# A two-layer hybrid encoder on one core: shared q and k roots, S5 work moved from GpSimd to VectorE, a bias negated on ScalarE, and one SBUF offset for the large buffers

## The chip, the cores and the metric

The kernel runs on one core of a Trainium2 chip. The metric is the device time of one execution in microseconds (us), as the median of the runs shown. The engines are named as the profile names them: PE (TensorE matmul), PEld (its weight loads), DVE (VectorE), ACT (ScalarE), POOL (GpSimd), SP (SyncE, which issues the DMAs). The span is the time from the first to the last instruction of the profiled execution.

## The reference, cut to what matters

Two layers, each a feed-forward block (FFN), a mixer and another FFN, on 512 tokens of width 1024, in float32:

```python
for layer in range(DEPTH):
    x = x + 0.5 * swiglu(rms_norm(x, ffn1_norm[layer]), ffn1_w_in[layer], ffn1_w_out[layer])
    x = x + hybrid_mixer(rms_norm(x, mix_norm[layer]), w_in[layer], ...)
    x = x + 0.5 * swiglu(rms_norm(x, ffn2_norm[layer]), ffn2_w_in[layer], ffn2_w_out[layer])
```

The mixer projects the normed x once and gives the columns to four groups: A (windowed attention, 4 query and 2 key heads), B (a bidirectional S5 scan over 16 groups with 64 complex states each, then a gate), C (dilated attention, 4 heads) and D (neighbourhood attention with a learned relative bias, 4 heads). A, C and D normalise each 64-wide head of q and k by its root mean square. The four outputs are multiplied by `w_out` and added to x.

```python
o_a, lse_a = banded_attention(rms_norm(heads(aq), qk_gain[0]), rms_norm(heads(ak), qk_gain[1]), heads(av), ...)
y_b = s5_bidirectional(bu, lam_re, lam_im, log_step, b_re, b_im, c_re, c_im, d_skip)
g = jax.nn.gelu(y_b)
y_b = g * jax.nn.sigmoid(g @ w_glu)
o_c = dilated_attention(rms_norm(heads(cq), qk_gain[2]), rms_norm(heads(ck), qk_gain[3]), heads(cv), ...)
o_d = neighborhood_attention(rms_norm(heads(dq), qk_gain[4]), rms_norm(heads(dk), qk_gain[5]), heads(dv), rel_bias)
return concat([o_a, y_b, o_c, o_d]) @ w_out
```

## The kernel before, in words

**Tiling.** The 512 tokens lie along the free dimension, features on the 128 partitions. Every float32 operand of a large matmul is split into a high and a low part, and `mm3` (L106 to L109) makes three matmuls of one product: low weight by high data or the other way round (L107, L108), and high by high (L109). A weight tile `wr` (up to 128x1024) is loaded by SP; `weights` (L118) splits it into `wh` (a cast on ACT, L125) and `wl` (a subtraction, L126, on DVE in the FFNs and on POOL in the mixer, where it is called with `pooled`).

**The FFNs.** The normed input is in eight pairs `hh`, `hl` (high, low). `pgp` and `pup` are the gate and up products into PSUM, `a` is the activated pair, `pop` the product with the output weights.

**The mixer.** `project` makes the 256-column blocks of the projection (`ppr`, 128x256 per matmul) from `wh`, `wl` and `hh`, `hl`; `ppt` is the transposed product for S5's input u and D's v. `qk` is one of six streams (dq, dk, cq, ck, aq, ak). Its fourth step ends in `norm`: ACT copies the block to `q` (L575) and squares it to `sq` (L579), DVE sums per head into `ss` (L580), adds epsilon (L583), takes 1/sqrt in `rsqrt` (L137; eleven small operations of 128x16, L140 to L145, three rounds of L143, L144, L145) and multiplies `q` by it (L589, four times 128x256). The fifth step, `flip`, transposes `q` on PE (`ptp`, L599); ACT scales and copies the result as the high part `o` (L606, L608), DVE makes the low part (L613, `kl` for k). `attention` has a first step (scores `psc` on PE, L687 and L688; bias and row minimum on DVE, L690; exp on ACT, L692; the division on POOL, L704) and a second (transposes L723, `pT` on ACT and DVE, L725 and L726, products `pot`, L728 and L729). After two heads, `m` is split into the pair `mt`: high on ACT (L746), low on POOL (L747). `merge` multiplies `mt` by the output weights (`pop`, L107 to L109) and DVE adds to `x` (L769). `d_bias` loads one head's bias for D (SP, L787) and makes mask minus bias of it with three DVE operations (L794).

**S5.** `s5` is a generator with a `yield` after each step: input rotation (`per`, `pei`, L818; two halves), scans (L833, L835), output rotation (L842 to L847, two halves; the products `rot` of L843 and L846 are on POOL, the other four on DVE), output matmuls `pyp` (L857 to L859, two halves of 24), and the gate (`gsp`, `pzp`, `mt` at L895).

**What sets the order.** `ORDER` (L35) is a list of tokens that gives the order in which steps are written: `dq` is the next step of stream dq, `Ds` and `Dt` the next halves of D's `first` and `second`, `s5` the next step of the generator, `mD` a step of the merge of D. Each step's instructions go to the engines' queues, and each queue runs in its order. A scheduler sets the final order from the written one, so the order on an engine is not read from the list alone. PSUM gives 3 banks to products (`mm`), 2 to scores and S5 (`sc`), 2 to transposes (`tp`) and 1 to `pot`.

## Time and profile before

| | before |
|---|---|
| median of 3 runs | 2018.51 us (2018.3 to 2020.4) |
| the profiled execution's own time | 2017.22 us |
| its span | 2015.4 us |
| mean granted clock of PE | 0.989 of full speed |
| PE busy | 1954.5 us (97%) |
| DVE, ACT, POOL busy | 1238.3, 801.1, 368.3 us |
| DMA | 189.5 MB, mean 94 GB/s |

Both layers have the same course. In the first, FFN 1 takes the span up to about 388 us, the mixer 388 to 643 us, FFN 2 the rest up to about 985 us; the second follows some 1000 us later. Times of places below are microseconds from the start of the span. An engine is busy while an instruction of it runs; matmuls overlap, so that a busy PE is one that never runs dry and not one at its peak rate.

### The profile page before, as it was taken

The page shows a single profiled execution, that of the slowest core. Times are in us where ns is not written, and L with a number is a line of the kernel's source. Part 1 is how long each engine was busy: PE and PEld are TensorE (multiplying, and loading weights), DVE is VectorE, ACT ScalarE, POOL GpSimd, SP SyncE. Part 2 cuts the span into 40 slices and gives each one's busy share as a digit, 9 for nine tenths or more (in the row PEclk, how much of TensorE's full clock was granted, in tenths as well). Part 3 has the DMA queues.
Part 4 walks back from the last instruction along what each step waited for, and adds up shares of the span by engine and source line. Part 5 has one row for each costly group of instructions (what it writes and reads, how often), then busy time and mean ns, then how long its engine had stood idle before and what let it go on. Part 6 is the DMA issues. An engine that isn't in the chain of part 4 may idle for free.

```text
span 2015.4 us, 25901 instructions
## 1 busy us (share of the span) xinstructions
PE 1954.5 (97%) x9656; PEld 1639.0 (81%) x9656; DVE 1238.3 (61%) x2317; ACT 801.1 (40%) x1515; POOL 368.3 (18%) x349
## 2 busy tenths in 40 slices
PE   8999999998999999999999999999989989999999
PEld 6788878897977888888888888788978768888887
DVE  6865547567797545445677655465787875444454
ACT  5333323453676323233432333234537753232332
POOL 4010100254455000000120101003544540000000
PEclk9999999998999999999999999999989999999999
DMA  4233343331312332323233332423313122333233
GB/s 177 81 102 91 105 94 101 99 116 47 98 55 72 102 97 92 102 84 110 84 116 92 99 93 94 107 90 106 112 45 93 50 71 89 100 96 102 81 108 104
DMA packets 75471, 189.50 MB, mean 94 GB/s; under 512 B 17984, under 2 KB 23872, under 8 KB 75344
## 3 DMA queue, kind: packets, MB, share of 16 engines
q1 hardware_dynamic: 75248, 187.77, 30.7%
q8 instruction: 76, 1.25, 0.3%
q14 instruction: 51, 0.42, 0.1%
q0 software_dynamic: 96, 0.07, 0.0%
...
## 4 chain that ended last, share of the span: by engine, by line
PE 81%; DVE 10%; ACT 4%; issue 2%; DMA 1%; POOL 1%; SPq 0%; DVEq 0%; ACTq 0%; POOLq 0%
PE pop L107 9%; PE pop L109 9%; PE pop L108 8%; PE pgp L107 7%; PE pgp L109 7%; PE pgp L108 7%; PE pup L107 7%; PE pup L109 7%; PE pup L108 7%; PE ppr L107 1%; PE ppr L108 1%; DVE wl L126 1%; PE ppr L109 1%; DMA wr<-in_f_w 1%; DVE hl L186 1%
## 5 line engine op out<-in xcount | busy, mean ns | idle before, releaser
L125 ACT CAST wh<-wr 128x512 fp32r<-128x512 f32 (+2 forms) x718 | 405.2, 570 | 962.6 <-PE pgp L109 306.4
L126 DVE TENSOR_TENSOR wl<-wr,wh 128x512 fp32r<-128x512 f32 (+2 forms) x618 | 408.6, 665 | 383.6 <-ACT wh L125 381.9
L107 PE MATMUL pop<-a,wl 128*128 128x512 f32 x704 | 277.9, 397 | 7.0 <-DVE wl L126 6.8
L107 PE MATMUL pgp<-hh,wl 128*128 128x512 f32 x704 | 275.3, 391 | 8.4 <-DVE wl L126 8.4
L107 PE MATMUL pup<-hh,wl 128*128 128x512 f32 x704 | 275.6, 392 | 2.7 <-DVE wl L126 2.7
L108 PE MATMUL pgp<-hl,wh 128*128 128x512 f32 x704 | 275.7, 392 | 2.5 <-DVE hl L186 2.4
L109 PE MATMUL pop<-a,wh 128*128 128x512 f32 x704 | 276.9, 393 | 0.0
L108 PE MATMUL pop<-a,wh 128*128 128x512 f32 x704 | 275.1, 391 | 0.6 <-DVE a L257 0.6
L109 PE MATMUL pup<-hh,wh 128*128 128x512 f32 x704 | 274.8, 390 | 0.0
L108 PE MATMUL pup<-hl,wh 128*128 128x512 f32 x704 | 274.8, 390 | 0.0
L109 PE MATMUL pgp<-hh,wh 128*128 128x512 f32 x704 | 274.4, 390 | 0.0
L196 POOL TENSOR_TENSOR t<-t,sq 128x512 f32<-128x512 f32 x42 | 60.0, 1430 | 658.2 <-ACT sq L195 656.9
L107 PEld LDWEIGHTS pop<-a,wl 128*128 128x128 f32 x704 | 132.6, 188 | 37.1 <-DVE wl L126 9.2
L107 PEld LDWEIGHTS pgp<-hh,wl 128*128 128x128 f32 x704 | 132.4, 188 | 36.4 <-DVE wl L126 8.8
L108 PEld LDWEIGHTS pgp<-hl,wh 128*128 128x128 f32 x704 | 132.4, 188 | 34.4 <-DVE hl L186 7.3
L126 POOL TENSOR_TENSOR wl<-wr,wh 128x512 fp32r<-128x512 f32 (+1 forms) x100 | 131.0, 1315 | 160.6 <-ACT wh L125 122.9
L107 PEld LDWEIGHTS pup<-hh,wl 128*128 128x128 f32 x704 | 132.4, 188 | 32.3 <-DVE wl L126 4.8
L109 PEld LDWEIGHTS pop<-a,wh 128*128 128x128 f32 x704 | 132.6, 188 | 30.5
L108 PEld LDWEIGHTS pop<-a,wh 128*128 128x128 f32 x704 | 132.6, 188 | 30.1 <-DVE a L257 1.0
L109 PEld LDWEIGHTS pup<-hh,wh 128*128 128x128 f32 x704 | 132.3, 188 | 27.6
L108 PEld LDWEIGHTS pup<-hl,wh 128*128 128x128 f32 x704 | 132.3, 188 | 27.6
L109 PEld LDWEIGHTS pgp<-hh,wh 128*128 128x128 f32 x704 | 132.3, 188 | 27.3
...
## 6 DMA issues: line engine op xcount, KB each, us to landing
...
bias<-in_ctab SPq DMA_DIRECT2D x8, 448.0 KB, 3.3
bias<-in_rbx SPq DMA_DIRECT2D x8, 448.0 KB, 4.1
...
```

Source lines behind the costliest of these rows:

```text
L107: nc.tensor.matmul(out, ll, rh, start=start, stop=False)
L108: nc.tensor.matmul(out, lh, rl, start=False, stop=False)
L109: nc.tensor.matmul(out, lh, rh, start=False, stop=stop)
L125: nc.scalar.copy(hi[:, :w], r)
L126: (nc.gpsimd if pooled else nc.vector).tensor_tensor(lo[:, :w], r, f32(hi[:, :w]), op=ALU.subtract)
L186: stt(hl, x[c], gcol, f32(hh), op0=ALU.mult, op1=ALU.subtract)
L196: gtt(acc, acc, sq, op=ALU.add)
```

## The change

What it does:

- `rsqrt` works on one flat tile of up to 32 columns. Of a pair (dq and dk, cq and ck, aq and ak) the `norm` of q ends at the sums; the `norm` of k adds its own sums beside them, takes one root for both (32, 32 and 24 columns) and multiplies q's and k's rows by it. `flip` of q therefore stands behind `norm` of k.
- In S5's output rotation the two products `rot` of each half (L843, L846) move from POOL to DVE, and so does the low part of `mt` (L747).
- `d_bias` no longer subtracts on DVE. The mask is in the loaded table as −1e30, and ACT negates the tile in one 128x896 operation (L802 of the changed kernel). The tile `dmask` and its load go.
- In `ORDER` S5's output matmuls come later and some steps of dq, aq, mD, mB and mC move.
- Before all other tiles, dummy tiles named `lay` and the eight x tiles are allocated in an order which puts all the large buffers (t2, k4, s8, wr, wh, wl, hh, hl, x) at addresses of 128 bytes above a multiple of 2048 in each partition. Before, wr and x lay at 992, t2, hh, hl, wh and wl at 1536, and k4 and s8 (which hold `a`, `mt`, `o`, `kl`, `pT`, `v`) at 1600 above one.

The number of matmul rows on PE is the same but for six; DVE has 68 fewer rows, POOL 21 fewer, ACT 6 more, SP as many. The core of the diff:

```diff
 ORDER = """
-dq dq dq dk dk dq dq dk s5 dk dv cq dk s5 Ds dv dv ck cq ck Ds cq dv Ds dv Ds Ds s5 cq s5 Dt ck s5 Dt s5 Dt ck
-cq s5 Ds cv Dt aq cv s5 aq Ds Dt Dt Ds ck Cs cv Dt s5 cv aq ak aq Cs s5 ak Dt Cs aq Cs Ct ak mD ak Cs Ct Cs Cs
-Ct ak Cs Ct s5 mD Ct mD As Ct As Ct Ct As mD As As At As As mB At As At At At mC mC mB mB mC At At mC At mC mC
+dq dq dq dk dk dq dk s5 dk dq dv cq dk s5 Ds dv dv ck cq ck Ds cq dv Ds dv Ds Ds s5 cq s5 Dt ck s5 Dt s5 Dt ck
+cq Ds cv Dt s5 aq cv aq s5 Ds Dt Dt Ds ck Cs cv Dt s5 cv aq ak aq Cs s5 ak Dt Cs Cs Ct ak mD ak aq Cs Ct Cs Cs
+Ct ak Cs s5 Ct mD Ct As Ct As Ct Ct As mD As As At As As mD At As At mB At At mB mB mC mC mC At At mC At mC mC
 mC mB mC mA mA
 """
...
+    t2("lay")
+    k4([P, 1024], name="lay")
+    s8([P, 2048], name="lay")
+    for tag, cols in (("wr", 1024), ("wh", 512), ("wl", 512), ("hh", 512), ("hl", 512)):
+        pool.tile([P, cols], F32 if tag == "wr" else F32R, tag=tag, bufs={"wr": 2, "hh": 8, "hl": 8}.get(tag, 4), name=nm(tag))
+    x = [pool.tile([P, S], F32, name=f"x{c}") for c in range(KC)]
...
-                sn = ss[:, :, :nh]
-                tt(sn, sn, bc(ec, 2, nh), op=ALU.add)
-                rn = sml([P, 4, 4], "rn")
-                rsqrt(rn[:, :, :nh], sn, [4, nh])
-                for j in range(2):
-                    for b in range(2):
-                        a = raw[j][:, b].rearrange("p (h d) -> p h d", d=64)
-                        tt(a, a, bc(rn[:, 2 * j + b, :nh], 2, 64), op=ALU.mult)
+                tt(ss, ss, bc(ec, 2, nh), op=ALU.add)
+                pair["raw"].append((raw, nh, o0))
+                if gi % 2 == 0:
+                    return
+                n = o0 + 4 * nh
+                rn = sml([P, 32], "rn")
+                rsqrt(rn[:, :n], pair["ss"][:, :n], n)
+                for rows, heads, o in pair["raw"]:
+                    rv = rn[:, o:o + 4 * heads].rearrange("p (b h) -> p b h", b=4)
+                    for j in range(2):
+                        for b in range(2):
+                            a = rows[j][:, b].rearrange("p (h d) -> p h d", d=64)
+                            tt(a, a, bc(rv[:, 2 * j + b], 2, 64), op=ALU.mult)
...
-                    gtt(mt[:, 1], m, f32(mt[:, 0]), op=ALU.subtract)
+                    tt(mt[:, 1], m, f32(mt[:, 0]), op=ALU.subtract)
...
-            for c0, m0, nk in ((0, 0, 2), (256, 2, 3), (640, 5, 2)):
-                bv = b[:, c0:c0 + nk * P].rearrange("p (k u w) -> p k u w", u=8, w=16)
-                tt(bv, bc(dmask[:, m0:m0 + nk], 2, 8), bv, op=ALU.subtract)
+            act(b[:, :896], b[:, :896], AF.Copy, scale=-1.0)
...
-                gtt(a, cz(si, gs), cz(T["s"], gs), op=ALU.mult)
+                tt(a, cz(si, gs), cz(T["s"], gs), op=ALU.mult)
...
-                gtt(b, cz(sr, gs), cz(T["s"], gs), op=ALU.mult)
+                tt(b, cz(sr, gs), cz(T["s"], gs), op=ALU.mult)
```

How it moves instructions. The first place is PE at the first scores of D in layer 0, where dk's transposes (`ptp` from `q_3656` before, `q_3624` after) come ahead of the scores `psc`. Before:

```order
1942 L599 MATMUL ptp_3758<-ident,q_3661 128x2x4x16
1943 L818 MATMUL pei_3774<-u_3323,s_624 128x64
1944 L107 MATMUL ppt_3694<-hh_3119,wl_3576 128x512
...
1955 L109 MATMUL ppt_3694<-hh_3153,wh_3575 128x512
1956 L107 MATMUL ppr_3717<-wh_3690,hl_3052 128x256
...
1967 L109 MATMUL ppr_3718<-wh_3690,hh_3085 128x256
1968 L687 MATMUL psc_3806<-o_3748,o_3554 128x256
1969 L687 MATMUL psc_3812<-o_3748,o_3554 128x384
```

and of the changed kernel:

```order
1967 L108 MATMUL ppr_3710<-wl_3683,hh_3091 128x256
1968 L109 MATMUL ppr_3710<-wh_3682,hh_3091 128x256
1969 L609 MATMUL ptp_3735<-ident,q_3624 128x2x4x16 x2
1970 L609 MATMUL ptp_3735<-ident,q_3629 128x2x4x16 x2
1971 L609 MATMUL ptp_3750<-ident,q_3624 128x2x4x16 x2
1972 L609 MATMUL ptp_3750<-ident,q_3629 128x2x4x16 x2
1973 L697 MATMUL psc_3796<-o_3740,o_3661 128x256
1974 L697 MATMUL psc_3802<-o_3740,o_3661 128x384
1975 L698 MATMUL psc_3796<-kl_3741,o_3661 128x256
1976 L698 MATMUL psc_3802<-kl_3741,o_3661 128x384
1977 L697 MATMUL psc_3931<-o_3740,o_3661 128x384
...
1981 L107 MATMUL ppt_3834<-hh_3014,wl_3702 128x512
```

The 12 `ppt` and 12 `ppr` that stood between dk's transposes and the scores stand ahead of the transposes now.

The second place is ACT at the same point; `o` are the scaled copies of the transposes, `a` the copy of a `ppt` bank, `wh` the weight casts of later projections. Of the changed kernel:

```order
280 L616 ACTIVATE o_3740<-ptp_3735,qkg 64x512
281 L618 ACTIVATE o_3740<-ptp_3735,qkg 64x512
282 L802 ACTIVATE bias_3791<-bias_3791 128x896
283 L616 ACTIVATE o_3755<-ptp_3750,qkg 64x512
284 L618 ACTIVATE o_3755<-ptp_3750,qkg 64x512
285 L802 ACTIVATE bias_3998<-bias_3998 128x896
286 L658 COPY a_3820<-ppt_3686 128x512
287 L702 ACT_TABLE_LOAD
...
291 L702 ACTIVATE p_3940,ll_3795<-p_3940,mn_3794 128x256
292 L802 ACTIVATE bias_4047<-bias_4047 128x896
293 L125 CAST wh_3849<-wr_3847 128x512
```

The negations of the first three heads' biases (L802) are new here, between the copies and ahead of the casts; before, the queue went from the copies `o` and `a` straight to the exponentials and casts.

The third place is DVE at the a pair's root, which the changed kernel runs between two additions of D's merge to `x` (L779, the former L769):

```order
664 L779 TENSOR_TENSOR x_72<-pop_5029,x_72 128x512
665 L585 TENSOR_REDUCE ss_4840<-sq_5077 128x4
666 L587 TENSOR_TENSOR ss_4840<-ss_4840,ec_3320 128x8
667 L700 ISA p_5129,mn_5124<-psc_5126,bias_5122 128x512
...
669 L139 TENSOR_SCALAR rn_5081<-ss_4840 128x24
670 L140 TENSOR_SCALAR rn_5081<-rn_5081 128x24
671 L142 TENSOR_TENSOR rq_5082<-rn_5081 128x24
...
678 L143 SCALAR_TENSOR_TENSOR rq_5082<-rq_5082,ss_4840 128x24
679 L779 TENSOR_TENSOR x_73<-pop_5302,x_73 128x512
680 L144 SCALAR_TENSOR_TENSOR rn_5081<-rq_5082,rn_5081 128x24
```

Rows 669 to 678 are ten operations of the root. The next product on PE, `pop_5310`, waits for row 679: the gate's two `pzp` hold the other two product banks. Before, the root of ak alone stood among the additions, with one of them and two `pT` between its operations.

## Rows read from the trace of the kernel before

**Rows 1.** The page: busy time, and the chain that ended last.

```profile
PE 1954.5 (97%) x9656; PEld 1639.0 (81%) x9656; DVE 1238.3 (61%) x2317; ACT 801.1 (40%) x1515; POOL 368.3 (18%) x349
...
PE 81%; DVE 10%; ACT 4%; issue 2%; DMA 1%; POOL 1%; SPq 0%; DVEq 0%; ACTq 0%; POOLq 0%
```

**Rows 2.** Stretches: length, busy time (count) of PE, PEld, DVE, ACT, POOL, clock, DMA.

```profile
300.00:350.00 50.00, 50.00 (x222) 41.36 (x221) 35.55 (x80) 16.28 (x27) 0.00 (x0) 1.00 0.33 104
...
450.00:500.00 50.00, 41.32 (x279) 39.51 (x278) 39.04 (x64) 19.43 (x45) 22.75 (x24) 0.86 0.16 53
```

**Rows 3.** Waits of PE in the mixer of layer 0: total, times, longest.

```profile
PE pyp L859 <- DVE zi L847: 5.7, 1, 5.7
PE pot L729 <- DVE pT L726: 2.9, 4, 1.2
...
PE pop L107 <- ACT mt L895: 1.6, 1, 1.6
PE pop L108 <- POOL mt L747: 1.2, 2, 0.9
```

**Rows 4.** PE at S5's output: start, us; in brackets the idle time before.

```profile
487.50 0.69 PE L859 MATMUL pyp<-zi,s 128*128 128x64 f32 x2 [5.68 <-DVE zi L847]
```

**Rows 5.** DVE in order of time there: start, us, line, output and inputs.

```profile
480.90 1.23 DVE L141 TENSOR_SCALAR rn<-rn 128x16 int32<-128x16 int32 x1
...
484.61 1.19 DVE L145 SCALAR_TENSOR_TENSOR rn<-rq,rn 128x16 f32<-128x16 f32 x1
485.83 0.17 DVE L143 TENSOR_TENSOR rq<-rn 128x16 f32<-128x16 f32 x1
486.04 0.17 DVE L144 SCALAR_TENSOR_TENSOR rq<-rq,ss 128x16 f32<-128x16 f32 x1
...
486.76 0.68 DVE L847 TENSOR_TENSOR zi<-zi,rot 128x512 f32<-128x512 f32 x1
```

**Rows 6.** POOL in order of time in the same stretch.

```profile
480.80 1.30 POOL L846 TENSOR_TENSOR rot<-sr,k 128x512 f32<-128x512 f32 x1
...
484.51 1.25 POOL L846 TENSOR_TENSOR rot<-sr,k 128x512 f32<-128x512 f32 x1
```

**Rows 7.** The stretch at the lower clock.

```profile
485.60:502.60 17.00, 15.10 (x71) 15.03 (x72) 9.78 (x26) 6.33 (x11) 0.16 (x1) 0.50 0.04 14
```

**Rows 8.** ACT in order of time at D's first scores.

```profile
438.18 0.69 ACT L606 ACTIVATE o<-ptp,qkg 64x512 fp32r<-64x512 f32 x1 [2.90 <-PE ptp L599]
438.88 0.69 ACT L608 ACTIVATE o<-ptp,qkg 64x512 fp32r<-64x512 f32 x1
...
444.46 0.59 ACT L648 COPY a<-ppt 128x512 f32<-128x512 f32 x1
```

**Rows 9.** PE in the same stretch.

```profile
437.65 0.61 PE L599 MATMUL ptp<-ident,q 128*128 128x128 f32 x4
...
438.23 0.47 PE L107 MATMUL ppt<-hh,wl 128*128 128x512 f32 x1
...
442.51 0.46 PE L687 MATMUL psc<-o,o 128*128 128x256 f32 x2
```

**Rows 10.** Groups by line and shape: count, busy us, mean ns, idle before.

```profile
L747 POOL TENSOR_TENSOR mt<-m,mt 128x512 fp32r<-128x512 f32 x12 | 16.4, 1364 | 33.2 <-ACT mt L746 33.2
...
L144 DVE SCALAR_TENSOR_TENSOR rq<-rq,ss 128x16 f32<-128x16 f32 x30 | 12.1, 404 | 0.8
```

**Rows 11.** DMA issues: count, KB, median us to landing.

```profile
bias<-in_rbx SPq DMA_DIRECT2D x8, 448.0 KB, 4.1
```

**Rows 12.** PE in FFN 2 of layer 0, first and last of 65 matmuls in sequence.

```profile
692.70 0.39 PE L109 MATMUL pup<-hh,wh 128*128 128x512 f32 x1
...
707.20 0.39 PE L107 MATMUL pgp<-hh,wl 128*128 128x512 f32 x1
```

**Rows 13.** PE there, first and last of 64 matmuls in sequence.

```profile
912.55 0.39 PE L109 MATMUL pop<-a,wh 128*128 128x512 f32 x1
...
926.97 0.39 PE L109 MATMUL pop<-a,wh 128*128 128x512 f32 x1
```

More of the change, by code (lines that the diff above doesn't have):

```diff
@@ L134, in weights, with rsqrt @@
         return at
-    def rsqrt(y, v, shape):
-        w = sml([P, 16], "rq")
-        w = w[:, :shape[0]] if len(shape) == 1 else w.rearrange("p (a b) -> p a b", a=shape[0])[:, :, :shape[1]]
+    def rsqrt(y, v, n):
+        w = sml([P, 32], "rq")[:, :n]
         yi = y.bitcast(I32)
@@ L156, in hybrid_encoder @@
     nc.sync.dma_start(gains, t["gains"])
-    x = []
     warm = pool.tile([P, 2], F32, name="warm")
@@ L160, in hybrid_encoder @@
     for c in range(KC):
-        xc = pool.tile([P, S], F32, name=f"x{c}")
-        nc.sync.dma_start(xc, t["xt"][c])
-        x.append(xc)
+        nc.sync.dma_start(x[c], t["xt"][c])
         if c == 0:
@@ L168, in hybrid_encoder @@
     sink = pool.tile([P, DEPTH, 4], F32, name="sink")
-    dmask = pool.tile([P, 7, 16], F32, name="dmask")
-    for tl, nme in ((qkg, "qkg"), (sink, "sink"), (dmask, "dmask")):
+    for tl, nme in ((qkg, "qkg"), (sink, "sink")):
         nc.gpsimd.dma_start(tl, t[nme])
@@ L560, in then, with qk @@
             return ld, go
-        def qk(blk0, nh, perm, gi, res, extra=None):
+        def qk(blk0, nh, perm, gi, res, pair, extra=None):
             st, steps = project(blk0)
@@ L570, in norm @@
                     extra(pts)
-                ss = sml([P, 4, 4], "ss")
+                if gi % 2 == 0:
+                    pair["ss"] = sml([P, 32], "ss")
+                    pair["raw"] = []
+                o0 = 16 * (gi % 2)
+                ss = pair["ss"][:, o0:o0 + 4 * nh].rearrange("p (b h) -> p b h", b=4)
                 for j in range(2):
@@ L900, in mixer @@
         dqk, dv, cqk, cv, aqk, av = [], [], [], [], [], []
+        pd, pc, pa = {}, {}, {}
         streams = {
-            "dq": qk(2, 4, 1, 4, dqk), "dk": qk(4, 4, 1, 5, dqk), "dv": v_perm(6, dv),
-            "cq": qk(8, 4, 0, 2, cqk), "ck": qk(10, 4, 0, 3, cqk), "cv": v_proj(12, cv),
-            "aq": qk(14, 4, 0, 0, aqk), "ak": qk(16, 2, 0, 1, aqk, lambda pts: av.append(v_split(pts, 128, 2))),
+            "dq": qk(2, 4, 1, 4, dqk, pd), "dk": qk(4, 4, 1, 5, dqk, pd), "dv": v_perm(6, dv),
+            "cq": qk(8, 4, 0, 2, cqk, pc), "ck": qk(10, 4, 0, 3, cqk, pc), "cv": v_proj(12, cv),
+            "aq": qk(14, 4, 0, 0, aqk, pa), "ak": qk(16, 2, 0, 1, aqk, pa, lambda pts: av.append(v_split(pts, 128, 2))),
             "s5": s5(), "mD": merge("woD", mt_d, 2), "mB": merge("woB", mt_b, 2), "mC": merge("woC", mt_ca, 3),
@@ L971, in _tables @@
         ctab[i] = np.where(mult > 0, slopes[4 + i] * dist - np.log(np.maximum(mult, 1)), BIG)
-    dmask = np.zeros((P, 7, 16), np.float32)
+    seen = np.zeros((P, 896), bool)
     ri = np.zeros((P, 896), np.int64)
@@ L975, in _tables @@
     r, c = np.arange(P) // 16, np.arange(P) % 16
-    for qb, k0, k1, col, m0 in ((0, 0, 2, 0, 0), (1, 0, 3, 256, 2), (3, 2, 4, 640, 5)):
+    for qb, k0, k1, col in ((0, 0, 2, 0), (1, 0, 3, 256), (3, 2, 4, 640)):
         qc = 16 * qb + c
@@ L983, in _tables @@
                     j = col + (kb - k0) * P + u * 16 + w
-                    dmask[:, m0 + kb - k0, w] = np.where((kc >= ws) & (kc < ws + 16), 0.0, BIG)
+                    seen[:, j] = (kc >= ws) & (kc < ws + 16)
                     ri[:, j] = u - r + 7
                     ci[:, j] = np.clip(kc - qc + 15, 0, 30)
-    return atab, ctab, dmask, ri, ci
+    return atab, ctab, seen, ri, ci
 def _layout(i):
@@ L1049, in _layout @@
     a["s5d"] = sd.reshape(DEPTH, P, 2 * P)
-    a["atab"], a["ctab"], a["dmask"], ri, ci = _tables()
-    a["rbx"] = ac(np.asarray(i["na_rel_bias"])[:, :, ri, ci])
+    a["atab"], a["ctab"], seen, ri, ci = _tables()
+    a["rbx"] = ac(np.where(seen, np.asarray(i["na_rel_bias"])[:, :, ri, ci], np.float32(-BIG)))
     return a
```

3 lines of the change are left out of this document (2 added, 1 removed).

## The prediction

> **What bounds the kernel now.** I read the page first. PE is busy for 97% of the span and holds 81% of the chain that ended last [rows 1]; DVE, at 61%, is next, so work taken off DVE, ACT or POOL counts only where PE waits for it. Then the stretches [rows 2]: in an FFN stretch PE never runs dry (50.00 of 50), in the mixer stretch 450 to 500 it is busy for 41.32 us, and its granted clock is 0.86. So the room is in the mixer. Then PE's waits there [rows 3]: one is large, 5.7 us for S5's `zi`, and many are short: 2.9 us in four waits for `pT`, 1.6 us for the gate's `mt`, 1.2 us in two for POOL's `mt`. The order of time shows the large one: PE starts `pyp` at 487.5 after 5.68 us in which it did nothing [rows 4]. DVE makes `zi` L847 only at 486.76, since it works through a root first, whose small operations take 1.19 to 1.23 us each up to 485.8 and 0.17 us afterwards [rows 5]. In the slow stretch POOL runs back to back, 1.25 to 1.30 us an instruction [rows 6], and one small DVE operation fits to each. Right behind the wait stands the last piece: from 485.6 to 502.6 PE's clock is 0.50, that is 1.2 GHz, with PE busy for 15.10 of the 17 us [rows 7]. Layer 1 repeats all this, so each term below counts twice.
>
> **The sum.** It is made against the profiled execution, 2017.2 us (span 2015.4 and 1.8 around it), which lies 1.3 us under the median of 2018.5; I add the difference to the median. All terms are per layer until the last.
>
> *S5's wait.* In the changed order `pyp` comes later on PE, `rot` needs no POOL, and the root of dq and dk is past. The 5.7 us go: −5.7. As to the slow root operations: the Trainium skill, SBUF — State Buffer, section SBUF: two separate sides, says that VectorE and GpSimd hold a shared port pair for a whole instruction and that the other one fully blocks meanwhile; the 1.2 us beside POOL and 0.17 us without it agree. It would make every root short if POOL were idle, but POOL keeps the weight splits (`wl` L126), so I do not count on it.
>
> *The clock.* At 2.4 GHz the 15.10 us of work would take 7.5 us. If the clock holds, that is −7.5; if it falls again elsewhere for as long, 0. The waits that I price next are as long as the one that goes, in front of other matmuls. I take the middle, −3.8.
>
> *D's first scores.* Before, 12 `ppt` and 12 `ppr` stood between dk's transposes and the first `psc`: from 438.23 to 442.51, 4.3 us of work [rows 9], in which ACT made six copies `o` (0.70 us from start to start [rows 8], 4.2 us). Now the scores follow the transposes at once. Count from the first of dk's eight transposes, at an estimated 0.11 us each, somewhat under a fourth of the 0.61 that four of them take with the last one's tail [rows 9]. (a) The first score needs two copies: 0.44 + 2 × 0.70 = 1.84 us, PE is through at 0.88: a wait of 1.0. (b) The third `psc` needs a bank, so DVE's minimum over the first, so the negated bias. The negation L802 is behind six copies (4.66 us), and no row shows a 128x896 operation on ACT. `a` with 512 columns takes 0.59 us [rows 8]; two of that are its upper bound, 1.2, one is the lower. I take 0.95, nearer to 896/512 of 0.59 (1.03) than to one. With an estimated 0.5 for DVE's minimum (`zi` with 512 columns takes 0.68), the bank is free at 6.1; PE, through the first four score matmuls (some 0.6), stands since 2.5: a wait of about 3.5. (c) The next `ppt` needs a bank of which ACT makes copy `a`, behind two more copies and the second negation: 4.66 + 0.95 + 1.4 + 0.95 + 0.6 = 8.6; PE, through the next four and a short wait for the second bank, is there at 7.0: 1.6. (d) The third bias uses the tile of the first, free at some 10; its load takes 4.1 us to land [rows 11], the negation 0.95, and the weight casts of the next `ppr` are queued behind on ACT, with POOL's `wl` of 1.3 after the cast: 10 + 4.1 + 0.95 + 0.6 + 1.3 = 17.0, against PE at 8.6 + 24 × 0.227 = 14.1: 2.9. Together 9.0; I take +8.5, with 6.0 (the load early) and 10 as the ends.
>
> *The `pT` stretch.* Between S5's scans and the next scores DVE gets four `rot` at 0.68 us (the time of `zi` L847 [rows 5]), and one `mt` split in the place of POOL's: 3.4 us in front of `pT`s which PE awaits already (2.9 us [rows 3]); and the 48 `pyp`, which lay among the `pot` and covered such waits, go elsewhere. I take +4, with 0 and 6 as ends.
>
> *The a pair.* DVE has ten root operations ahead of the addition that frees the bank of the next `pop`. Beside an idle POOL that is 10 × 0.21 + 0.6 = 2.7 us (0.21 from start to start, 485.83 to 486.04 [rows 5]), beside a busy one 10 × 1.2 + 0.6 = 12.6. PE has eight 128x512 matmuls in the meantime, 1.8 us. Bounds 0.9 and 10.8. The mean of such an operation over the run is 0.40 us [rows 10], nearer to the short end: two slow and eight short make 2.4 + 1.7 + 0.6 = 4.7, and with the bank's hand-over I take +3.3.
>
> *The gate and the merge of B.* S5's output is some 54 `ppr` later (6.5 us), and the second and third step of mB now stand two `At` steps behind the first, where six and two mC steps stood before. The wait for the gate's `mt` is 1.6 us now [rows 3]. I take +3.5 on top, with 0 and 5 as ends.
>
> *`mt`'s split.* On POOL it takes 1.36 us [rows 10], on DVE 0.69: each of the two waits for it (1.2 us together [rows 3]) shrinks by half: −0.6.
>
> *D's bias on DVE.* The 24 subtractions of a run go, and three of six roots of a layer. DVE is not the bound; what they gain lies in the terms above. The `dmask` load, first in the run, hides behind the FFN: 0.
>
> Per layer −5.7 − 3.8 + 8.5 + 4 + 3.3 + 3.5 − 0.6 = +9.2; twice, +18.4.
>
> *The one offset.* 65 matmuls on `hh`, `hl` take (707.20 − 692.70)/64 = 226.6 ns each [rows 12], 64 on `a` take (926.97 − 912.55)/63 = 228.9 ns [rows 13]. The one visible difference of their operands is where they lie: 1536 bytes above a multiple of 2048, or 1600. No row shows 128. If all go as the first, 2112 `pop` on `a` and 384 on `mt` gain 2.3 ns each, −5.7; if all as the second, 4224 gate and up products and some `ppr` lose as much, +10. 128 is a multiple of 128 as 1536 is, and 1600 is not, so I take −5. By the Trainium skill, TensorE: Matmul & The Clock Gate, section Back-to-back issue gap, a matmul of 512 columns takes 512/2.4 + 2.5 = 216 ns from start to start, whatever its operands' place: the trace has 227 to 229. By that rule, with no effect of the place, this term would be 0 and the sum +18.4.
>
> In all +13.4: 2018.5 + 13.4 = 2032 us, slower by 0.66%. With each term at its ends the case reaches from about no change to +50; its own likely range is 2022 to 2050.
>
> **The rivals.** *A: the stall goes, and what replaces it is covered.* It ends on the other side. The mechanism is DVE's queue in the mixer: it loses three of six roots a layer, over both layers 6 × 11 × 0.40 = 26 us [rows 10], and the bias. If by that the additions and `pT`s come early, the terms of the `pT` stretch and of B are 0, the a pair's is 0.9, the short waits for `pT` and `mt` go as well (−4), and the clock holds (−7.5). The term at D's first scores cannot be covered, because ACT's row is fixed, but the load can be early (6.0). Per layer −5.7 − 7.5 + 6.0 + 0.9 − 4 − 0.6 = −10.9, twice −21.8, with the offset −27: 1992 us. It decides from the point at which the a pair's root runs beside an idle POOL and no wait in the `pT` stretch is above 0.5 us. For it speaks the 0.17 us row, against it that PE's waits in the page are for DVE already. Chance 0.27.
>
> *B: the parts cancel.* The clock holds (−7.5 in the place of −3.8) and B's merge and the `pT` stretch cost half: −5.7 − 7.5 + 8.5 + 2 + 3.3 + 1.7 − 0.6 = +1.7, twice +3.4, less 5: 2017 us. Chance 0.10.
>
> *C: the offset is worth much more.* The 226.6 ns hold a share that the old places cost, and at 128 it goes. If each of the 6912 matmuls of 512 columns (4224 gate and up, 2112 and 384 `pop`, 192 `ppt`) lost the 2.3 ns between the two rows twice over, that would be −32 us, and with the sum of +18.4, 2005 us. The skill's 216 ns, if it is the place that the trace's 227 lacks, would make it about −73 us and the time 1964. That hh and `a` differ by 1% only speaks against a large effect. Chance 0.03.
>
> **How the numbers follow.** The forecast has a chance of 0.60, A 0.27, B 0.10, C 0.03. The time is the forecast's, 2032. A measurement of this kernel can tell about 0.2%, 4 us, from no change: faster is A, C and a little of B, 0.31; same is most of B, 0.09; slower is the forecast, 0.60. The range reaches up to 2050, the forecast's own upper end (about 0.06 beyond), and down to 1988, which takes in the larger part of A and leaves out C's far end and A's lower part (0.13).
>
> **What would show it.** Right: no wait before `pyp`; in its place two or three waits at D's first scores of 1, 3.5 and 1.6 us, for ACT's `o`, DVE's minimum and ACT's `a`, then one for `wh`; a wait of 3 us in front of a `pop` at D's merge, released by the addition to `x`; the FFN stretches with 221 to 223 matmuls in 50 us as now. Wrong: PE's busy time in the mixer stretches above 47 of 50 throughout and no stretch at half clock (A); another count of matmuls in the FFN stretches (C, or the offset's sign); or a wait at D's first scores that is short because the negation is much below 0.95 us or stands early enough in time.

## The result, and the profile after

The changed kernel takes 2047.71 us (2046.19 to 2048.88, 4 runs) against 2019.45 us for the kernel before in the same comparison: ratio 1.014, 95% interval 1.0128 to 1.0153, slower by 28 us. The forecast was +13.4 us, 2032: the sign was right, the size less than half of what came. The profiled execution took 2046.19 us with a span of 2044.3, 28.9 more than before, and all sums below are made against that.

The page of the changed kernel, busy time and chain (for [rows 1]):

```profile
PE 1958.0 (96%) x9656; PEld 1636.9 (80%) x9656; DVE 1206.4 (59%) x2247; ACT 808.5 (40%) x1523; POOL 340.6 (17%) x328
...
PE 82%; DVE 9%; ACT 3%; issue 3%; DMA 2%; POOL 1%; SPq 0%; ACTq 0%; POOLq 0%; DVEq 0%
```

DVE lost 32 us of work and POOL 28, ACT has 7 more. PE's busy time is 3.5 us longer over the whole span and the count of its instructions the same: the 29 us are mostly PE's idle time. Where they lie is read from the stretches; first the two mixers of the changed kernel, then those of the kernel before (length, busy time of PE, PEld, DVE, ACT and POOL, granted clock, DMA share, GB/s):

```profile
389.60:659.60 270.00, 240.24 (x1524) 211.08 (x1523) 172.97 (x364) 148.59 (x315) 110.07 (x123) 0.96 0.26 79
1403.10:1673.60 270.50, 240.63 (x1524) 211.18 (x1523) 172.98 (x365) 148.20 (x314) 110.08 (x123) 0.96 0.24 75
```

```profile
387.80:643.10 255.30, 237.28 (x1525) 213.11 (x1524) 187.19 (x399) 144.52 (x310) 123.42 (x133) 0.96 0.27 82
1388.40:1643.40 255.00, 237.02 (x1524) 212.85 (x1523) 189.88 (x399) 144.44 (x310) 123.78 (x133) 0.96 0.25 79
```

The mixers are 14.7 and 15.5 us longer, which is more than all of the 28.9; the rest of the span is 1.3 us shorter. In both layers PE's idle time makes most of that (29.8 for 18.0 us in the first) and its busy time some 3 (240.24 for 237.28). The mean clock of a mixer is 0.96 in both kernels: PE spends 20.5 us of each at 1.2 GHz before and after (a mean of 0.96 lacks 0.04 × 255 = 10.2 us of full speed, and each microsecond at half clock lacks half of one: 20.4). What differs most is who PE waits for. The waits of the changed kernel in the first mixer, for [rows 3] (total, times, longest):

```profile
PE psc L697 <- DVE mn L700: 6.1, 7, 2.8
PE pop L107 <- ACT mt L756: 4.1, 2, 2.3
PE pop L107 <- DVE x L779: 3.5, 3, 2.4
PE pop L107 <- ACT mt L903: 3.3, 1, 3.3
PE pot L739 <- DVE pT L736: 2.8, 4, 1.1
PE ppr L107 <- ACT q L580: 1.4, 2, 0.7
PE pot L738 <- DVE m L749: 1.2, 1, 1.2
PE pot L738 <- DVE m L753: 1.2, 1, 1.2
PE ppt L107 <- ACT a L658: 1.1, 1, 1.1
PE psc L697 <- ACT o L618: 1.0, 1, 1.0
...
```

All rows of this view add up to 29.5 us in 32 waits; before, to 17.9 in 18. S5's wait for `zi` is gone, as forecast, and 17 us of others have come. Two of the three order excerpts ahead of the prediction can be seen at work. First D's scores, PE, then ACT, then DVE in order of time (start, us, in brackets the idle time before):

```profile
444.89 1.32 PE L609 MATMUL ptp<-ident,q 128*128 128x128 f32 x8
447.21 0.56 PE L697 MATMUL psc<-o,o 128*128 128x256 f32 x2 [1.00 <-ACT o L618]
...
451.46 0.69 PE L697 MATMUL psc<-o,o 128*128 128x384 f32 x1 [2.84 <-DVE mn L700]
...
453.98 0.79 PE L107 MATMUL ppt<-hh,wl 128*128 128x512 f32 x1 [1.09 <-ACT a L658]
```

```profile
445.79 0.68 ACT L616 ACTIVATE o<-ptp,qkg 64x512 fp32r<-64x512 f32 x1
...
449.99 0.95 ACT L802 ACTIVATE bias<-bias 128x896 f32<-128x896 f32 x1
...
452.37 0.95 ACT L802 ACTIVATE bias<-bias 128x896 f32<-128x896 f32 x1
453.34 0.58 ACT L658 COPY a<-ppt 128x512 f32<-128x512 f32 x1
```

```profile
450.97 0.42 DVE L700 CUSTOM_DVE_ANT_0 p<-psc,bias 128x256 f32<-128x256 f32 x1 [0.22 <-ACT bias L802]
```

Six copies of 0.70 us from 445.79 to 449.99, the negation of 0.95, then DVE's minimum, and PE's bank is free: this is the chain of the prediction, step by step, with waits of 1.00, 2.84 and 1.09 us where 1.0, 3.5 and 1.6 were forecast. In the middle of it PE's clock falls, in the first of the four half-clock stretches of this mixer. Two stood there before, that of [rows 7] and one of 3.4 us. The columns are those above; first the stretch that the rows ahead of the prediction do not show, then the four of the changed kernel:

```profile
618.70:622.10 3.40, 3.40 (x15) 3.10 (x14) 1.25 (x3) 1.02 (x3) 1.17 (x1) 0.50 0.00 0
```

```profile
450.00:456.90 6.90, 4.36 (x11) 3.48 (x12) 4.02 (x11) 6.78 (x12) 0.00 (x0) 0.51 0.18 56
494.40:497.80 3.40, 3.40 (x19) 3.40 (x18) 3.40 (x8) 2.00 (x4) 0.00 (x0) 0.50 0.00 0
590.00:596.80 6.80, 5.50 (x13) 4.30 (x14) 4.29 (x6) 2.22 (x4) 4.15 (x3) 0.50 0.00 0
654.80:658.20 3.40, 3.40 (x9) 2.62 (x8) 1.59 (x3) 0.73 (x2) 0.00 (x0) 0.50 0.30 122
```

Second the a pair. DVE in order of time, POOL beside it, and PE at its wait:

```profile
562.56 0.62 DVE L140 TENSOR_SCALAR rn<-rn 128x24 int32<-128x24 int32 x1
563.22 1.23 DVE L142 TENSOR_TENSOR rq<-rn 128x24 f32<-128x24 f32 x1
564.48 1.21 DVE L143 SCALAR_TENSOR_TENSOR rq<-rq,ss 128x24 f32<-128x24 f32 x1
565.72 0.18 DVE L144 SCALAR_TENSOR_TENSOR rn<-rq,rn 128x24 f32<-128x24 f32 x1
...
566.91 0.68 DVE L779 TENSOR_TENSOR x<-pop,x 128x512 f32<-128x512 f32 x1
```

```profile
563.12 2.53 POOL L126 TENSOR_TENSOR wl<-wr,wh 128x512 fp32r<-128x512 f32 x2
```

```profile
564.82 0.39 PE L698 MATMUL psc<-kl,o 128*128 128x512 f32 x1
567.65 0.50 PE L107 MATMUL pop<-mt,wl 128*128 128x512 f32 x1 [2.44 <-DVE x L779]
567.99 0.40 PE L108 MATMUL pop<-mt,wh 128*128 128x512 f32 x1
```

The root's operations take 1.21 to 1.23 us each until POOL's two subtractions end at 565.65, and 0.18 us from 565.72 on, as in [rows 5]; the addition to `x` comes last. Forecast +3.3, measured 2.44 here and 3.5 for all waits for `x`.

The last rows show what a wait costs besides its idle time. The matmul ahead of it counts 0.39 us, since no other overlaps its end, and from the one behind it to the next pass 0.34 us; in sequence, 227 ns pass from start to start. So each wait adds some 0.16 + 0.11 = 0.27 us to PE's busy time. The mixer has 14 waits more than before: 3.8 us a layer by this estimate, which is about the growth of PE's busy time (3.0 and 3.6 us).

### The profile page after: what moved, and what is told of

Read it like the earlier page. It is cut to its first block, busy times and chain, and to the rows that moved or that the text cites. A ratio compares the mean times of both kernels' runs of the same rounds, so it can differ in the third digit from the quotient of the medians.

```text
span 2044.3 us, 25854 instructions
## 1 busy us (share of the span) xinstructions
PE 1958.0 (96%) x9656; PEld 1636.9 (80%) x9656; DVE 1206.4 (59%) x2247; ACT 808.5 (40%) x1523; POOL 340.6 (17%) x328
## 4 chain that ended last, share of the span: by engine, by line
PE 82%; DVE 9%; ACT 3%; issue 3%; DMA 2%; POOL 1%; SPq 0%; ACTq 0%; POOLq 0%; DVEq 0%
PE pop L107 9%; PE pop L109 9%; PE pop L108 9%; PE pgp L108 7%; PE pup L107 7%; PE pgp L109 7%; PE pgp L107 7%; PE pup L109 7%; PE pup L108 7%; PE ppr L107 2%; PE ppr L108 2%; PE ppr L109 2%; DVE wl L126 1%; DMA wr<-in_f_w 1%; DVE hl L187 1%
```

## The experiments

All times are medians; before was run beside each (2018.3 to 2019.75 us). "Clock" is the mean granted clock of a kernel's runs. "Waits" is the sum of PE's waits view over one mixer, "half" the time of that mixer at 1.2 GHz; they and the mixers' lengths are of the profiled execution, first and second layer (which took 2015.6 us for b_nopool and 2006.1 for b_lay_rot, more than their medians).

| run | us | ratio to before (95%) | clock | mixers, us | waits, us | half, us |
|---|---|---|---|---|---|---|
| before | 2019.5 | | 0.989 | 255.3, 255.0 | 17.9, 18.0 | 20.5, 20.5 |
| after | 2047.7 | 1.0128 to 1.0153 | 0.987 | 270.0, 270.5 | 29.5, 29.6 | 20.5, 20.5 |
| b_layout | 2014.2 | 0.9960 to 0.9982 | 0.990 | 255.1, 255.2 | 17.9, 17.8 | 20.5, 20.5 |
| b_lay64 | 2012.9 | 0.9958 to 0.9982 | 0.989 | 255.4, 255.0 | 17.7, 17.9 | 20.5, 20.5 |
| b_nopool | 2010.6 | 0.9938 to 0.9973 | 0.992 | 259.2, 248.2 | 16.4, 16.2 | 30.7, 3.4 |
| b_neg | 2019.6 | 0.9994 to 1.0011 | 0.989 | 254.8, 254.9 | 19.2, 19.4 | 17.1, 17.1 |
| b_order | 2025.5 | 1.0019 to 1.0043 | 0.992 | 259.3, 258.6 | 21.4, 21.6 | 17.1, 13.7 |
| b_order_np | 2030.2 | 1.0040 to 1.0066 | 0.988 | 262.8, 261.1 | 21.6, 22.3 | 27.3, 17.1 |
| b_order_neg | 2026.5 | 1.0026 to 1.0050 | 0.991 | 260.0, 259.1 | 21.8, 21.8 | 17.1, 17.1 |
| b_lay_np | 2009.1 | 0.9921 to 0.9958 | 0.991 | 259.2, 248.2 | 16.4, 16.2 | 30.7, 3.4 |
| b_lay_np_neg | 2007.4 | 0.9929 to 0.9956 | 0.992 | 252.7, 252.9 | 18.5, 18.2 | 13.7, 13.7 |
| b_lay_rot | 1998.9 | 0.9888 to 0.9922 | 0.990 | 251.1, 251.3 | 12.1, 12.2 | 23.9, 23.9 |
| l_flip | 2026.7 | 1.0025 to 1.0049 | 0.984 | 262.8, 262.5 | 19.7, 19.3 | 30.7, 30.7 |
| l_s5 | 2020.2 | 0.9994 to 1.0012 | 0.992 | 259.3, 257.6 | 22.6, 21.1 | 13.7, 13.7 |
| l_merge | 2017.1 | 0.9983 to 1.0000 | 0.992 | 257.2, 256.6 | 23.0, 23.1 | 13.7, 10.2 |
| p_min | 2044.4 | 1.0099 to 1.0146 | 0.982 | 267.1, 266.2 | 25.2, 25.4 | 27.3, 23.9 |
| a_unpair | 2037.2 | 1.0077 to 1.0105 | 0.987 | 266.0, 267.8 | 26.5, 26.9 | 23.9, 23.9 |
| a_cover | 2034.3 | 1.0062 to 1.0086 | 0.989 | 266.5, 266.2 | 25.5, 26.1 | 20.5, 20.5 |
| a_max | 2045.5 | 1.0119 to 1.0146 | 0.984 | 270.4, 270.8 | 27.2, 27.6 | 27.3, 23.9 |
| a_oldneg | 2051.6 | 1.0152 to 1.0180 | 0.984 | 273.4, 274.1 | 30.7, 31.5 | 27.3, 27.3 |

A thousandth of the clock is 4 us of a run of 2020 at half speed, some 1.6 us of time at the price found below (0.40 us for each, an estimate). So a few microseconds between two medians can be the clock's alone; the waits beside them tell more of the order of work.

**The parts alone, on the kernel before.** Theory 1: the list and the late flips make the loss. Theory 2: work moved onto the queues that PE waits for makes it.

b_layout:

```diff
+    t2("lay")
...
+    x = [pool.tile([P, S], F32, name=f"x{c}") for c in range(KC)]
```

> The kernel before with the one offset alone: the dummy tiles and x allocated first, nothing else. If matmuls on operands at 128 bytes above a multiple of 2048 go at the 226.6 ns of those at 1536 (rows 12), the 2112 pop on a and the 384 on mt gain 2.3 ns each: 5.7 us faster, and the pop in FFN 2 stand 226.6 ns apart. Rival: the place of an operand does not matter (a kernel with the same order of operations takes the same time, within 2 us), and the 228.9 ns have another cause.

Measured: 5.6 us faster, mixers unchanged, all of it outside them. The size of the offset's term holds; its reason is tested further down.

b_nopool:

```diff
-                    gtt(mt[:, 1], m, f32(mt[:, 0]), op=ALU.subtract)
+                    tt(mt[:, 1], m, f32(mt[:, 0]), op=ALU.subtract)
...
-                gtt(a, cz(si, gs), cz(T["s"], gs), op=ALU.mult)
+                tt(a, cz(si, gs), cz(T["s"], gs), op=ALU.mult)
...
-                gtt(b, cz(sr, gs), cz(T["s"], gs), op=ALU.mult)
+                tt(b, cz(sr, gs), cz(T["s"], gs), op=ALU.mult)
```

> The kernel before with the two rot products of S5's output and mt's low part on DVE, nothing else. Theory 1 (the order and the late flips make the loss): S5's wait of 5.7 us shrinks to 2 or less because DVE's small root operations no longer meet POOL's rot, so 4 to 10 us faster over both layers. Theory 2 (work moved onto the queues that PE waits for makes the loss): DVE's pT and x come later, 6 us slower or more.

Measured: 9.1 us faster, against theory 2. But most of it is not S5's wait: that shrank to 1.3 us, others grew, and a mixer's waits fell by only 1.5 and 1.8. The mean clock, 0.992 for 0.989, makes some 6 us of the 9.1 by the price just given. The six runs, 2005.0 to 2015.8 us, follow the granted clock, 0.996 for the fastest and 0.988 for the slowest; at 0.990 it took 2015.6 us, where before took 2017.1 and 2017.5 at the same clock. Its two mixers are the most telling pair of the study. PE has the same matmuls there, in the same order but for the last 90 or so, ahead of which the whole difference has come about; the mixers wait 16.4 and 16.2 us, and one is 11.0 us longer:

```profile
393.40:652.60 259.20, 242.49 (x1525) 216.94 (x1524) 187.09 (x410) 146.43 (x312) 112.03 (x124) 0.94 0.26 82
1394.40:1642.60 248.20, 231.60 (x1525) 206.09 (x1523) 186.27 (x410) 146.23 (x312) 113.14 (x124) 0.99 0.26 82
```

What differs is the clock, 0.94 against 0.99: 30.7 us at half speed against 3.4. So 27.3 us more at the lower clock cost 11.0 − 0.2 us, 0.40 us each. That S5's wait is short does not keep the clock up: the first layer has it short and has 30.7 us at half speed, where before has 20.5.

b_neg:

```diff
-                tt(bv, bc(dmask[:, m0:m0 + nk], 2, 8), bv, op=ALU.subtract)
+            act(b[:, :896], b[:, :896], AF.Copy, scale=-1.0)
...
```

> The kernel before with D's bias masked in its table and negated on ACT (one 128x896 operation in the place of three on DVE), nothing else. Theory 1: before the first scores PE has 4.3 us of cover for ACT, the third score still waits for the negation behind six copies, some 1 to 2 us a layer; 0 to 4 us slower in all. Theory 2: the negations hold the copies and casts that PE needs, 6 us slower or more.

Measured: no difference. 1.3 us more of waits a layer, 3.4 us less at half clock.

b_order:

```diff
-dq dq dq dk dk dq dq dk s5 dk dv cq dk s5 Ds ...
+dq dq dq dk dk dq dk s5 dk dq dv cq dk s5 Ds ...
```

(all of the new list)

> The kernel before with the new ORDER list alone: separate roots, POOL's work, DVE's bias and the old places in SBUF stay. Theory 1: the list itself costs, since S5's output and the flips lose cover: 10 to 20 us slower. Theory 2: the list takes S5's wait of 5.7 us a layer away and costs nothing by itself: 5 to 12 us faster.

Measured: 5.8 us slower, between the two; its clock is 0.992 for 0.989, so that at the clock of before it would be some 5 us more (an estimate). Its waits show why theory 2's gain is missing:

```profile
PE pot L729 <- DVE pT L726: 9.4, 6, 5.8
PE psc L687 <- DVE mn L690: 3.0, 3, 1.1
PE ppt L107 <- ACT a L648: 1.9, 1, 1.9
```

The longest wait is still 5.8 us, but now a `pot` waits for `pT`: POOL's `rot` is still there, and what PE met at `pyp` it meets at another instruction that needs DVE.

**All but root and list; the root; the negation.**

b_lay_np_neg is b_layout, b_nopool and b_neg together.

> All of the change but the shared root and the new list: offset, DVE in POOL's place and the negation on ACT, on the kernel before. If the parts measured alone add up (-5.6, -9.1, 0): 15 us faster than before, 2005, and all of the loss lies in root and list. If the parts need the new list to pay, as a rival has it: within 5 us of before.

Measured: 2007.4, 11 us ahead of before: the parts nearly add, and all of the loss, 40 us against this run, comes with the list and the shared root.

a_unpair takes the changed kernel and gives it separate roots:

```diff
...
-            "dq": qk(2, 4, 1, 4, dqk, pd), "dk": qk(4, 4, 1, 5, dqk, pd), "dv": v_perm(6, dv),
+            "dq": qk(2, 4, 1, 4, dqk), "dk": qk(4, 4, 1, 5, dqk), "dv": v_perm(6, dv),
...
```

(and `norm` as in the kernel before)

> The changed kernel with a separate root for q and for k again; the list ORDER, the negation on ACT, DVE in POOL's place and the offset stay. Theory 3 (the shared root makes the loss: q's rows and transposes come a projection later, and k's norm carries the work of both just ahead of the scores): 15 to 25 us faster than the changed kernel, near 2027. Theory 4 (the negations on ACT under the new order make it): 0 to 5 us faster than the changed kernel, 2043 to 2047.

Measured: 10.5 us faster than after, less than theory 3 has it and more than theory 4. Taken off first, the shared root makes about a quarter of the 40 us; the list, with the negation and the rest in place, makes the other 29.7.

a_oldneg:

```diff
-            act(b[:, :896], b[:, :896], AF.Copy, scale=-1.0)
+                tt(bv, bc(dmask[:, m0:m0 + nk], 2, 8), bv, op=ALU.subtract)
...
```

> The changed kernel with D's bias made by three DVE subtractions from dmask again; shared root, list, DVE in POOL's place and offset stay. Theory 4: the 4.9 us of waits a layer at D's first scores (for o, the minimum and the copy a) fall to 2 or less, 8 to 15 us faster than the changed kernel, 2033 to 2040. Theory 3: the waits stay, now for DVE's subtractions; within 4 us of 2048.

Measured: 3.9 us slower than after. The negation on ACT is not the loss; with the subtractions on DVE the waits grow by 1.2 to 1.9 us a layer, and the half clock by 6.8.

a_max:

```diff
-    for i in (0, 2, 4):
+    for i in (0, 2):
         ts(qkg[:, :, i], qkg[:, :, i], -1.0, None, op0=ALU.mult)
         ts(qkg[:, :, i + 1], qkg[:, :, i + 1], 8.0, None, op0=ALU.mult)
...
-                                                   op1=ALU.min, accum_out=mn[:, b:b + 1])
+                                                   op1=ALU.max if up else ALU.min, accum_out=mn[:, b:b + 1])
+                    if up:
+                        ts(mn[:, b:b + 1], mn[:, b:b + 1], -1.0, None, op0=ALU.mult)
...
-            act(b[:, :896], b[:, :896], AF.Copy, scale=-1.0)
```

> The changed kernel with no bias operation at all: the masked table is added as it is, q's gain of D is not negated, DVE takes a maximum in the place of a minimum, and one DVE operation of 128x1 negates it ahead of the exponential, 32 a run. Theory 4: 8 to 15 us faster than the changed kernel. Theory 3: the third score's wait of 2.8 us and the wait of 1.1 us for a go, the rest stays: 3 to 8 us faster, 2040 to 2045.

With the sign of q's gain the edit also leaves out the factor of 8 on k's, the second line of that loop, so that D's scores are an eighth of the reference's; the kernel serves for its time alone. Measured: 2.2 us faster than after, less than both theories. Waits fall by 2 us a layer, and the half clock grows by 6.8 and 3.4.

**The list in pieces, on b_lay_np_neg (2007.4).**

l_flip:

```diff
-dq dq dq dk dk dq dq dk s5 dk dv
+dq dq dq dk dk dq dk s5 dk dq dv
```

> The run with all of the change but shared root and list (2007.4 us), with the first piece of the new list: dq's last steps and its flip behind dk's, dk's flip right ahead of D's scores. List and negation together cost a run with separate roots 29.7 us against 2007.4; this splits the list. Theory F (the lost cover at D's first scores): the waits of 2.3 and 1.8 us for the minimum and for a, and the stretch at half clock behind them, come back here: 8 to 14 us slower, 2015 to 2021. Theory S (S5's output later): within 3 us.

l_s5:

```diff
-cq s5 Ds cv Dt aq cv s5 aq Ds
+cq Ds cv Dt s5 aq cv aq s5 Ds
...
-ak Cs Ct s5 mD Ct
+ak Cs s5 Ct mD Ct
```

> The same base (2007.4 us) with the second piece alone: S5's steps later in the list, dq, aq and merges as before. Theory S: the pot wait for pT (1.2, 1.6 and 1.0 us between 488 and 493) because pyp no longer stands among them, with the half clock behind it: 8 to 14 us slower. Theory F: within 4 us of the base.

l_merge:

```diff
-Dt Cs aq Cs Ct ak mD ak Cs Ct
+Dt Cs Cs Ct ak mD ak aq Cs Ct
...
-mD Ct mD As Ct As Ct Ct As mD As As At As As mB At As At At At mC mC mB mB mC At
+mD Ct As Ct As Ct Ct As mD As As At As As mD At As At mB At At mB mB mC mC mC At
```

> The same base with the third piece alone: aq's flip later, mD, mB and mC moved in the last line. Theory M (the last third of the mixer: waits for mt of 3.4 and 2.3 us and for x): 8 to 14 us slower. Theories F and S: within 4 us of the base. If none of the three pieces is above 5, it is their combination that costs.

Measured: +19.3, +12.8 and +9.7 us. Each piece costs, so theories F, S and M hold each in part; the sum of 41.8 is more than the 29.7 of all three. In l_flip the waits at D's scores are there again, but a layer's waits grow by only 1.2 us, and its half clock from 13.7 to 30.7, by 17.0: at 0.40 us each, 6.8 of the 10 us by which its mixer is longer: most of this piece's loss is the clock's. In l_s5 and l_merge the half clock is as in the base or less and the waits carry it (+4.1 and +2.9; +4.5 and +4.9).

p_min has the shared root and the two moves of the list that it needs, on the same base.

> The same base with the shared root and only those moves in the list that it needs: dq's flip behind dk's norm, aq's behind ak's; S5 and the merges stay. If the shared root costs by the late flips (theory 3): as l_flip and 8 to 12 us more, about the 10.5 that the root cost under the new list: 2024 to 2032. If the new list is what makes a shared root dear: within 6 us of l_flip.

Measured: 2044.4 (2035.0 us at a clock of 0.987 to 2052.2 at 0.978), 17.7 more than l_flip, above both forecasts: the shared root is dear without the rest of the new list as well, 5.5 and 6.1 us more of waits a layer.

**What interacts, and what the cover is worth.**

a_cover changes the list of the changed kernel at one place, so that `ppt` stand between dk's transposes and the scores again (18 in its trace, where 24 were expected: 5.0 us from the first transpose to the first score):

```diff
-cq dk s5 Ds dv dv ck cq ck Ds
+cq dk s5 dv dv Ds ck cq ck Ds
```

> The changed kernel with D's first score step two dv steps later in the list, so that 24 ppt stand between dk's transposes and the scores. If the waits there (1.0, 2.8 and 1.1 us a layer in the profile of the changed kernel) and the clock that falls behind them (6.8 us at half speed from 450) are lost for good, this gives them back: 10 to 16 us faster, 2032 to 2038. If they only move, because DVE and ACT are as late for the next step: within 5 us of 2048.

Measured: 13.4 us faster than after, in the forecast's range, but in part by luck: the half clock that was to come back did not (20.5 us a mixer in both). By the profiles the mixers give 3.5 and 4.3 us, with 4.0 and 3.5 less of waits, and the rest of the span 3.4, which was not traced. So of the 4.9 us of waits at D's first scores the larger part was a real loss, and it does not all come back elsewhere; its longest waits in the first mixer now:

```profile
PE psc L694 <- DVE mn L697: 4.6, 7, 2.1
PE pop L104 <- ACT mt L753: 4.4, 2, 2.6
PE pop L104 <- ACT mt L900: 3.3, 1, 3.3
```

b_order_np (list, and POOL's work on DVE):

```diff
...
-                gtt(b, cz(sr, gs), cz(T["s"], gs), op=ALU.mult)
+                tt(b, cz(sr, gs), cz(T["s"], gs), op=ALU.mult)
```

(the edit of b_nopool and the list of b_order)

> The kernel before with the new list and POOL's rot and mt on DVE; separate roots, DVE's bias, old places. The two alone gave +5.8 and -9.1. If they add: 2016. If the list needs POOL (work moved to DVE stands in front of the pT and x that PE awaits under the new list): 2026 or more.

b_order_neg (the list of b_order and the edit of b_neg)

> The kernel before with the new list and the negation on ACT; separate roots, POOL's work, old places. The two alone gave +5.8 and 0. If they add: 2025. If the negation costs under the new list, since no cover stands ahead of the scores: 2031 or more.

Measured: b_order_neg adds up (2026.5). b_order_np does not: 2030, where the sum is 2016. Its waits are those of b_order to 0.7 us; its half clock is 10.2 and 3.4 us longer. In the profiled executions (2017.2 us for before, 2015.6, 2026.2 and 2033.9) the two fall short of adding by 9.4 us. There b_nopool has 6.9 us less at half clock than before over both layers, and b_order_np 13.6 more than b_order, 8.2 us at 0.40 each; the waits, 3.3 us lower in b_nopool and 0.9 higher here, would be another 4.2. Clock and waits thus cover the 9.4, and by more than it, so the price is rough. The list costs 5.8 us on the kernel before, 19.5 with POOL's work on DVE (b_order_np against b_nopool), and 29.7 with the offset and the negation as well; what makes the last 10 was not tested.

b_lay_np (offset and POOL's work)

> The kernel before with the offset and with POOL's rot and mt on DVE, nothing else. If the two parts add (-5.6 and -9.1): 2005, faster than the kernel before by 0.7% and than the changed one by 2.1%. The run that had the negation too gave 2007.4.

Measured: 2009.1, 4 us above the sum, with a spread of 1999.1 us at a clock of 0.996 to 2013.9 at 0.988. Its profile has the uneven layers of b_nopool again.

**The last two.**

b_lay64:

```diff
+    nc.vector.memset(pool.tile([P, 16], F32, name="pad"), 0.0)
     t2("lay")
```

> The kernel before with all large buffers at one offset as in the change, but 64 bytes further (192 above a multiple of 2048), by a 64-byte tile ahead of them that is filled once. If a remainder of 64 by 128 is what made pop on a slow (228.9 against 226.6 ns), every matmul with hh, hl, a or mt is slow now: the gate and up products lose 4224 x 2.3 ns = 9.7 us, ppt and ppr up to 2 more, pop stays slow: 2029 to 2031, 15 or more above b_layout. If only the mixture of offsets counted, or 1600 by itself: as b_layout, 2014.

Measured: 2012.9, as b_layout. The rival holds: the remainder by 128 does not count. Whether the mixture of offsets did, or 1600 by itself, this run does not tell. First and last of 63 `pop` in sequence in FFN 2 of b_lay64, for [rows 13], and of 64 in the changed kernel:

```profile
912.74 0.39 PE L109 MATMUL pop<-a,wh 128*128 128x512 f32 x1
...
926.79 0.39 PE L108 MATMUL pop<-a,wh 128*128 128x512 f32 x1
```

```profile
929.65 0.39 PE L109 MATMUL pop<-a,wh 128*128 128x512 f32 x1
...
943.93 0.39 PE L109 MATMUL pop<-a,wh 128*128 128x512 f32 x1
```

(926.79 − 912.74)/62 = 226.6 ns and (943.93 − 929.65)/63 = 226.7 ns, against 228.9 before.

b_lay_rot (b_layout, and only the two `rot` on DVE):

```diff
...
-                gtt(a, cz(si, gs), cz(T["s"], gs), op=ALU.mult)
+                tt(a, cz(si, gs), cz(T["s"], gs), op=ALU.mult)
```

> The kernel before with the offset and S5's two rot products of each half on DVE; mt's low part stays on POOL. With both on DVE PE's waits for ACT's mt rose from 2.0 to 4.4 us a layer while S5's wait fell from 5.7 to 0.6. If mt on DVE is what raised them, rot alone keeps them at 2: 2000 to 2006, ahead of 2009.1 with both. If not: 2007 to 2012.

Measured: 1998.9 us, a ratio of 0.9905 (0.9888 to 0.9922): ahead of both kernels, by 1% and by 2.4%. S5's wait is down to two of 0.6 and 0.7 us and nothing as long has taken its place:

```profile
PE pot L732 <- DVE pT L729: 2.8, 4, 1.7
PE pop L107 <- ACT mt L749: 1.8, 1, 1.8
PE psc L690 <- DVE mn L693: 1.7, 3, 1.2
PE pop L107 <- ACT mt L898: 1.6, 1, 1.6
```

The wait for ACT's `mt` in the merges is 1.8 us, where b_nopool and b_lay_np have 4.4. At the same granted clock, 0.989, b_lay_rot took 2001.3 us and b_lay_np 2009.2. `mt`'s low part on DVE was the bad half of the move. Why it delays ACT's high part was not looked into further.

## Why the prediction was right or wrong

**The sign, and the mechanism of the forecast: right.** S5's stall went, waits at D's scores, at the a pair's addition and at B's merge came. a_cover shows that the term at D's scores is a loss on the path for the larger part; b_neg and b_nopool, that neither moved work as such makes it. Rival A is out: the waits for `pT` and for ACT's `mt` did not go (2.8 and 4.1 us), and the mixer keeps its 20.5 us at half clock. Of rival B the two halved terms came true (+2.2 and +1.6 for its 2 and 1.7), its clock did not. Rival C is out by the 222 matmuls that an FFN stretch of 50 us holds as before.

**The steps that failed: the clock, and the loss at each wait, which had no term.** The forecast took −3.8 us a layer for the clock, half of what the stretch [rows 7] would give back. That stretch went, but the clock fell in four others, each beside a wait that is new or longer: after the 2.84 us that end at 451.46, after four waits between 486.9 and 493.9, around the 3.26 us that end at 591.3 and after the 2.25 us that end at 654.5. So 20.5 us of each mixer are at half clock after as before. PE is busy for 16.7 of them in the first mixer and for 18.5 before, so that by the prediction's own rule, half of the busy time, 0.9 us came back at most. The prediction allowed for 0 and had no row that spoke for the middle. That the runs hold other values between 3.4 and 30.7 us a mixer, and b_nopool both of these with nearly the same waits, shows that the waits' length alone does not give this term.

The second step is a term put at nothing: the sum has PE's idle time at a wait, but not the 0.27 us that each wait adds to its busy time, 3.8 us a layer by the estimate above; measured are 3.0 and 3.6 us of longer busy time, with what little the clock gave back already taken off.

The sum was short by 15.5 us in all. Of that the mixers make 11.8 (30.2 for 18.4), per layer 3.8 that the clock did not give and 3.3 of longer busy time, less 1.4 by which the waits were priced too high; 0.2 is not placed. Another 3.7 lie outside the mixers: they shrank by 1.3 us where −5 was forecast and b_layout's did by 5.1. Here too the clock has a part. Up to PE's last matmul before has one stretch at half clock there, at 1294.5 (3.4 us), b_layout has none, and the changed kernel two, at 296 and 1310: between b_layout and the changed kernel some 2.7 of the 3.8 us, at 0.40 each, and 1.4 of b_layout's own 5.1. The rest is open.

**The waits of the sum: right in total by luck.** Without the clock the terms of a layer were −5.7 + 8.5 + 4 + 3.3 + 3.5 − 0.6 = +13.0, and the waits view grew by 11.6. By terms, in the first mixer:

- S5's wait: −5.7, as forecast.
- D's first scores: 5.2 us (with 0.3 for `kl`) where 0.4 was before, +4.8 and not +8.5. The prediction's parts (b) and (c) were 0.7 and 0.5 too high, and (d), 2.9, did not come. Its chain on ACT came as forecast: the third negation starts at 458.94, 14.05 us after the first transpose, forecast 14.1. But PE reached the `ppr` behind it only at 461.6, 16.7 us after it and not 14.1, since the first of the `ppt` run at half clock and four scores come first. The one wait for `wh`, 0.4 us, is elsewhere, at 538.
- The `pT` stretch: 3.4 us in four waits between 486.9 and 493.9, one of them for `m`, where 1.2 was before: +2.2 of 4.
- The a pair: +3.5, forecast +3.3.
- The gate's `mt`: 3.3 for 1.6, +1.6 and not +3.5.
- The split `mt`, forecast −0.6: POOL's 1.2 went, but the waits for ACT's `mt` rose from 2.0 to 4.1, +0.9.
- Without a price: the further waits for DVE's minimum (3.3 us besides the 2.8 at D's scores, 1.7 before: +1.6) and for ACT's `q` (2.3 for 0.7, +1.6), and some smaller ones.

The terms with a price came to 7.3 of 13.0: three were too high, by 7.4 us together, and `mt`'s split had the wrong sign. The waits that had no price, some 4 us, made up for most of that.

**The offset: right in size, wrong in reason.** −5.6 measured against −5; but b_lay64 has the same, so a multiple of 128 is not it. Before, `pop` read weights (`wh`, `wl`) at 1536 and data (`a`) at 1600; in the fast cases, `hh` before and everything in b_layout and b_lay64, both lie at the same remainder by 2048. That fits; with unequal offsets other than these two, or with both at 1600, it was not tried. The figure of the Trainium skill that was weighed there (TensorE: Matmul & The Clock Gate, section Back-to-back issue gap), 216 ns for 512 columns, is given in that section for a matmul by itself; for a stream of weight loads and matmuls, as this kernel is, the section has 131 ns. The trace shows neither: 227 ns, and 229 in one place.

**The lock between DVE and POOL** was read rightly: the root's operations were slow (1.21 to 1.23 us) until POOL's subtractions ended and short (0.18) from then on. Two slow and eight short ones were a guess from the mean of 0.40 us; it came out, and the a pair was priced to 0.2 us.
